# Two heads of a gated recurrence share one run of small matmuls, their starts are moved, and a later consumer takes three steps where it took four

## The chip, the cores and the metric

The kernel runs on one core of one Trainium2 chip. The metric is the device time in microseconds (us), the median of several runs; lower is better.

## The reference, cut to what matters

Two layers of a decoder trunk for a sequence of 256 tokens with 2048 features, in float32. Layer 0 mixes tokens with two mixers side by side, a gated MLP over chunks (gMLP, `y_a`) and a linear recurrence with forget gates (HGRN2, `y_b`); layer 1 is attention with forget gates; each layer ends in a gated MLP with a short convolution. The change touches layer 0's mixers alone:

```python
def hgrn2(q, f_logit, i, g, lower_bound, o_gain):          # 8 heads of 128
    log_f = logaddexp(log(lb), log1p(-lb) + log_sigmoid(fl))
    k = (1.0 - lb) * sigmoid(-fl)
    def step(state, xs):                                   # chunks of 64 tokens
        G = cumsum(lf_c, axis=2)
        o_inter = einsum('bhtk,bhkv->bhtv', q_c * exp(G), state)
        decay = exp(where(mask, G_t - G_s, -inf))
        scores = einsum('bhtk,bhtsk,bhsk->bhts', q_c, decay, k_c)
        o_intra = einsum('bhts,bhsv->bhtv', scores, v_c)
        new_state = exp(G_end) * state + einsum('bhsk,bhsv->bhkv', k_c * exp(G_end - G), v_c)
        return new_state, o_inter + o_intra
    return rms_norm(o, o_gain) * silu(g)

def mixer_ab(h, ...):
    u, v, q, f, i, g = split(h @ w_in, cuts)
    u, v = gelu(u), rms_norm(gelu(v), v_gain)
    mixed = einsum('hts,bcshd->bcthd', w_causal, v) + sp_b
    y_a = u * mixed
    y_b = hgrn2(q, f, i, g, lower_bound, o_gain)
    return concatenate([y_a, y_b]) @ w_out
```

## The kernel before

**Large products and steps.** Every weight matrix streams through the core once. `weights` (L190) loads a tile of 128 x 1024 numbers by SyncE's DMA queue into `w`, ScalarE rounds it into `wh` (L213), and VectorE subtracts to get the rest `wl` (L218). With the activations split the same way (`a`, later `ya` and `yb`), three matmuls of 512 columns take the place of one in full precision: L274 to L276 in `project_tok`, L294 to L296 in `project_four`. One such tile is twelve large matmuls on TensorE; this document calls it a step and numbers them from 1. There are four buffers of `w`, and three each of `wh` and `wl`, so ScalarE can be at most some two steps ahead of TensorE. The sums of a product lie in two PSUM banks (`pm`), one for each half of the tokens, and are evacuated by ScalarE when a product of eight steps is complete.

The order in layer 0: `w_v` (steps 1 to 16), then for each half of the heads `w_f`, `w_q`, `w_i` (eight steps each, to step 64), `w_u` (65 to 80), `w_g` (81 to 96), and the output product `w_abo` from step 97.

**Everything else rides along.** Work between the large products is written as Python generators. `tick()` (L138) runs once per step, ahead of its `weights`, and moves every live generator to its next `yield`; `after(n, g)` lets a generator begin n steps later; `start` begins one at once. So a `yield` is a step's wait, and what a generator records between two of them stands between the weight tiles of two steps in the engines' queues. A tile framework then orders the instructions of each engine and adds the semaphores; an engine executes its own in that order. `behind` and `add_manual_dep` hold an instruction behind another in that order without a semaphore. `mm_in` and `turn_in` are a matmul and a transpose on TensorE that stand behind the large matmuls handed over so far.

**A head of the recurrence, `hgrn(h)`** (L615). Instead of exponentials of sums it keeps products: the head's gates `l` and its keys and queries `t` (tile `kq`) are multiplied up level by level, for blocks of 1, 2, 4 ... 64 tokens. At each of the seven levels ScalarE copies the keys and queries as they stand into `E` (L633), and VectorE multiplies on (`kq`, `tot`; L637 to L644). The `yield`s in the loop spread this over three steps. Then on TensorE a cross product of two chunks (`xps`, 128 x 128) and two 64 x 64 products a level for the two groups of partitions (`levels`; one PSUM bank for even heads, one for odd). A step later ScalarE copies the cross product into `s128` (L659) and the first level into the head's state tile `st` (L662); VectorE masks the levels (`smk`, L664), sums them (`own`, L666), and writes `st` (L671). After some more steps a transpose of `st` on TensorE (L677 copies it out), and a step after that three products with the values `itok` (L166, L684, L685), whose squares, roots and scaled copies ScalarE and VectorE make (`so`).

`queries` (L694) starts the heads: for the j-th half and its i-th head it calls `after((4, 3)[j] * i + 1 - i // 2, hgrn(...))`; it has a `yield` behind every second head, so heads begin at its steps 1, 5, 9 and 13 in the first half, and 1, 4, 7 and 10 in the second.

**Around it.** `spatial(j, z)` (L754) is the gMLP: it waits until all eight heads are through (`left`), applies Gelu to the turned `w_u` product, and for each of four products multiplies and splits it into `ya`, with two `yield`s behind each. `gated` (L733) evacuates a `w_g` product with Silu into `zg`, multiplies by `itok`, and turns it with VectorE's transposes and 16 small DMAs into `yb`. `ya` and `yb` are what the output product reads.

ScalarE's functions come in tables; `act` loads one where the function's table is not the last one loaded (L98).

Of the kernel before, what the change touches and what calls it, by code (L numbers as in the profile page):

```python
# [11 lines left out]
AF = mybir.ActivationFunctionType  # L12
# [3 lines left out]
P = 128  # L16
HP = P // 2
# [17 lines left out]
AHEAD = {2: 2, 4: 4, 6: 6}  # L35
BEHIND = {6: 8, 8: 12}
LANE = 64
LEVELS = (64, 32, 16, 8, 4, 2, 1)
NL = len(LEVELS)
MCOLS = 2 * (NL + 1) * P  # L40
# [16 lines left out]
def tile_trunk(ctx: ExitStack, tc: tile.TileContext, x, pp_d, cst_d, mlev_d, msk_d,  # L57
               w_v, w_f, w_g, w_i, w_q, w_u, w_abo, w_cf, w_cqkv, w_cg, w_co, w_up, w_dn, spw_d, spb_d, out):
    nc = tc.nc
    V, SC, PE = nc.vector, nc.scalar, nc.tensor  # L60
# [15 lines left out]
    for c0, n in ((0, 1), (1, 1), (2, 1), (3, 1), (4, 2), (6, 2), (8, 4), (12, 4)):  # L76
        t = cp.tile([P, n, S], F32, tag=f"x{c0}", name=f"x{c0}")
        xload.append((t, c0, n))
        xT += [t[:, i] for i in range(n)]
    fetch = {c0: (t, x[:, c0:c0 + n, :]) for t, c0, n in xload}  # L80
    pp = cp.tile([P, -(-NPP // LANE) * LANE], F32, tag="pp", name="pp")
    cst = cp.tile([P, NK], F32, tag="cst", name="cst")
    ones = cp.tile([P, P], F32, tag="ones", name="ones")
    one1 = cp.tile([P, LANE], F32, tag="one1", name="one1")[:, 0:1]

# [6 lines left out]
    order = mybir.DependencyInfo(mybir.DependencyClass.NoSync, mybir.DependencyReason.DATA)  # L92
# [22 lines left out]
    def bank(tag="px"):  # L115
        n = nm(tag)
        return small["pool"].tile([P, 512], F32, tag=tag, name=n, bufs=small[tag])
# [22 lines left out]
    depth = [2]  # L140
# [6 lines left out]
    def after(n, g):  # L147
        soon.append([n, g])
# [16 lines left out]
    def mm_in(*args, **kw):  # L165
        return behind(PE.matmul(*args, **kw), "main")  # L166
# [179 lines left out]
    def rsq(dst, src, n):  # L346
        tag = "sq" if dst.shape[-1] == S else "rm"
        cols = dst.shape[-1] if dst.shape[-1] == S else LANE // math.prod(dst.shape[1:-1])
        m, t = (tp.tile(list(dst.shape[:-1]) + [max(cols, dst.shape[-1])], F32, tag=tag, name=nm(n_))
# [12 lines left out]
    class Norm:  # L362
# [30 lines left out]
        def finish_tok(self):  # L393
            p2 = bank()
            for T in range(2):
# [4 lines left out]
                yield  # L400
            Rt = cp.tile([P, LANE], F32, tag="Rt", name=nm("Rt"), bufs=2)[:, 0:2]
            rsq(Rt, p2[:, 0:4].rearrange("p (t two) -> p t two", two=2)[:, :, 0], D)
# [22 lines left out]
    def mixer_ab(norm):  # L425
# [3 lines left out]
        level = [bank("levels") for _ in range(2)]  # L429
# [60 lines left out]

        ss = hp.tile([P, LANE], F32, tag="ss", name="ss")

        def values():
# [7 lines left out]
            for li in range(1, NL):  # L501
                n = LEVELS[li]
                part = view(tri[:, 1], 0, (2 * n, 32 // n), (n - HP, 2), (1, n))
# [45 lines left out]
        gam = pp[:, C_GAM:C_GAM + 3 * NH]  # L549
        gm = hp.tile([P, LANE], F32, tag="gm", name="gm")  # L550
        mx, sm_, lb, omlb = (gm[:, i * NH:(i + 1) * NH] for i in range(4))
# [56 lines left out]
                yield  # L608

        yB = [None] * KT  # L610
        depth[0] = 3

        itoks, left = [], [NH]

        def hgrn(h):  # L615
            l, t = lf[h], kq[h]
            d0 = (h % 4) * P
            SC.activation(l, l, AF.Identity, bias=lb[:, h:h + 1], scale=omlb[:, h:h + 1])
            st = sts[h % 4]
            dg = hp.tile([P, 2, HP], F32, tag="dg", name=nm("dg"), bufs=4)  # L620
            V.tensor_tensor(dg, eye.unsqueeze(1).to_broadcast([P, 2, HP]),
                            dgc[:, h].unsqueeze(2).to_broadcast([P, 2, HP]), ALU.mult)
            yield

            V.tensor_tensor(t[:, 1::2], t[:, 1::2], view(l, P, (-P, 2), (1, P)), ALU.mult)
            E = hp.tile([P, NL, 2, P], F32, tag="E", name=nm("E"), bufs=2)
            tot = l
            tots = hp.tile([P, S], F32, tag="tot", name=nm("tot"), bufs=1)
            for li in reversed(range(NL)):
                n = LEVELS[li]  # L630
                m = P // n
                for sl in range(2):
                    SC.activation(E[:, li, sl].rearrange("p (b two n) -> p b two n", two=2, n=n),  # L633
                                  view(t, 2 * P * sl, (2 * n, 64 // n), (P + n, 2), (1, n)), AF.Copy)
                if not li:
                    ends = view(t, 0, (P + n, 2), (1, n))
                    V.tensor_tensor(ends, ends, view(tot, 1, (1, 2), (0, n)), ALU.mult)  # L637
                    break
                even = view(t, 0, (2 * P, 2), (2 * n, 64 // n), (1, n))
                odd = view(t, P + n, (2 * P, 2), (2 * n, 64 // n), (1, n))  # L640
                V.tensor_tensor(even, even, view(tot, 1, (m, 2), (2, m // 2), (0, n)), ALU.mult)
                V.tensor_tensor(odd, odd, view(tot, m, (-m, 2), (2, m // 2), (0, n)), ALU.mult)
                nt = tots[:, S - 2 * m:S - m]
                V.tensor_tensor(nt, view(tot, 0, (2, m)), view(tot, 1, (2, m)), ALU.mult)  # L644
                tot = nt
                if n in (4, 16):
                    yield
            yield
            xps = bank()
            mm_in(xps[:, 0:P], t[:, 0], t[:, 1], start=True, stop=True)  # L650
            i = h % 2
            for li in range(NL):
                for g in range(2):
                    k, q0 = slice(g * HP, (g + 1) * HP), (g if li else 1 - g) * HP
                    mm_in(level[i][k, li * HP:(li + 1) * HP], E[:, li, 0, k], E[:, li, 1, q0:q0 + HP],
                          start=True, stop=True)
            yield
            s128 = hp.tile([P, 2, P], F32, tag="s128", name=nm("s128"), bufs=2)
            SC.activation(s128[:, 0], xps[:, 0:P], AF.Copy)  # L659
            for g in range(2):  # L660
                k = slice(g * HP, (g + 1) * HP)
                SC.activation(st[k, g, HP - g * HP:P - g * HP], level[i][k, 0:HP], AF.Copy)  # L662
            smk = hp.tile([P, NL - 1, HP], F32, tag="smk", name=nm("smk"), bufs=1)
            V.tensor_tensor(smk, level[i][:, HP:NL * HP].rearrange("p (l c) -> p l c", l=NL - 1), msk, ALU.mult)  # L664
            own = hp.tile([P, HP], F32, tag="own", name=nm("own"))
            V.tensor_reduce(own, smk.rearrange("p l c -> p c l"), AX.X, ALU.add)  # L666
            both = smk[:, 0:2]
            V.tensor_tensor(both, own.unsqueeze(1).to_broadcast([P, 2, HP]), tri, ALU.mult)
            for g in range(2):
                k = slice(g * HP, (g + 1) * HP)  # L670
                V.tensor_tensor(st[k, :, k], both[k], dg[k], ALU.add)  # L671
            yield
            yield
            yield
            op = bank()
            turn_in(op[:, S:S + P], st[:, 1], ident)
            SC.activation(s128[:, 1], op[:, S:S + P], AF.Copy)  # L677
            yield
            while len(itoks) <= h // 4:
                yield  # L680
            itok = itoks[h // 4]
            i0, i1 = (itok[:, T, d0:d0 + P] for T in range(2))
            mm_in(op[:, 0:P], st[:, 0], i0, start=True, stop=True)
            PE.matmul(op[:, P:S], s128[:, 0], i0, start=True, stop=False)  # L684
            PE.matmul(op[:, P:S], s128[:, 1], i1, start=False, stop=True)  # L685
            so = hp.tile([P, LANE], F32, tag="so", name=nm("so"), bufs=2)[:, 0:2]
            for T in range(2):
                SC.activation(itok[:, T, d0:d0 + P], op[:, T * P:(T + 1) * P], AF.Square,
                              accum_out=so[:, T:T + 1])
            rsq(so, so, P)  # L690
            for T in range(2):
                SC.activation(itok[:, T, d0:d0 + P], op[:, T * P:(T + 1) * P], AF.Copy, scale=so[:, T:T + 1])
            left[0] -= 1

        def queries(j, z):
            while len(kq) < 4 * j + 4:
                yield
            for i in range(4):
                t = kq[4 * j + i]
                copy_in(view(t, 3 * P, (-2 * P, 2), (1, P)), natural(z[:, i]), AF.Copy)  # L700
                after((4, 3)[j] * i + 1 - i // 2, hgrn(4 * j + i))
                if i % 2:
                    yield

# [52 lines left out]
        def spatial(j, z):  # L757
            while left[0] or j and yB[4 * j - 1] is None:
                yield
            yield  # L760
            act_in(z, z, AF.Gelu)
            yield
            for i in range(4):
                b = 4 * j + i
                m = mg[b].rearrange("p (t n) -> p t n", t=2)
                sum_in(m, m, natural(z[:, i]), ALU.mult)
                yB[b] = quad("ya")
                split(yB[b], mg[b], turn=True)
                yield
                yield  # L770

        for j in range(2):
            after(LAG, spatial(j, turn(w_u[4 * j:4 * j + 4], late=True)))
# [477 lines left out]
```

## Time and profile before

| | |
|---|---|
| median of three runs | 2286.39 us (2286.0 to 2288.47) |
| the profiled execution's own time | 2287.58 us |
| its span, first to last instruction | 2285.8 us |
| TensorE (PE) busy | 2280.1 us |
| VectorE (DVE) busy | 1557.5 us |
| ScalarE (ACT) busy | 1315.6 us |
| GpSimd (POOL) busy | 421.2 us |
| mean granted TensorE clock | 1.000 |

How its lines are read. A row of the timeline has the start in us from the span's start, the duration in us, the engine, the line, the operation, what it writes `<-` what it reads, the shapes, how many such instructions follow each other (`x2`), and in brackets how long the engine was idle before it and what ended that wait. A row for a tile has the shortest, median and longest duration in ns. A row of a stage has its bounds and length, and then for each engine the busy us and the number of instructions, the granted clock, the DMA share and GB/s. A matmul in full precision shows as two passes. Matmuls overlap: their starts tell the pace, and their ends are modelled.

### The profile page before, as it was taken

The page shows a single profiled execution, that of the slowest core. Times are in us where ns is not written, and L with a number is a line of the kernel's source. Part 1 is how long each engine was busy: PE and PEld are TensorE (multiplying, and loading weights), DVE is VectorE, ACT ScalarE, POOL GpSimd, SP SyncE. Part 2 cuts the span into 40 slices and gives each one's busy share as a digit, 9 for nine tenths or more (in the row PEclk, how much of TensorE's full clock was granted, in tenths as well). Part 3 has the DMA queues.
Part 4 walks back from the last instruction along what each step waited for, and adds up shares of the span by engine and source line. Part 5 has one row for each costly group of instructions (what it writes and reads, how often), then busy time and mean ns, then how long its engine had stood idle before and what let it go on. Part 6 is the DMA issues. An engine that isn't in the chain of part 4 may idle for free.

```text
span 2285.8 us, 31588 instructions
## 1 busy us (share of the span) xinstructions
PE 2280.1 (100%) x10486; PEld 1895.1 (83%) x10486; DVE 1557.5 (68%) x2357; ACT 1315.6 (58%) x1973; POOL 421.2 (18%) x779
## 2 busy tenths in 40 slices
PE   9999999999999999999999999999999999999999
PEld 8888888888888888888888888888888888888887
DVE  7888667767467657766776675667776466667766
ACT  7578756656456445554555556655665455455642
POOL 0212232221012002201322211322311012012102
PEclk9999999999999999999999999999999999999999
DMA  8756677877667667765676656778777677666765
GB/s 282 217 171 195 198 217 217 243 223 216 201 194 233 208 202 217 214 215 175 186 232 211 194 178 193 209 224 242 224 218 218 195 210 217 208 210 212 223 203 175
DMA packets 487909, 481.07 MB, mean 210 GB/s; under 512 B 102880, under 2 KB 454640, under 8 KB 487744
## 3 DMA queue, kind: packets, MB, share of 16 engines
q1 hardware_dynamic: 460080, 448.42, 63.4%
q0 software_dynamic: 25360, 27.37, 5.0%
q10 hardware_dynamic: 2304, 3.26, 0.4%
q8 instruction: 82, 1.34, 0.3%
q14 instruction: 83, 0.68, 0.1%
HBM read 434.85 MB, written 2.12 MB: 191 GB/s over the span
## 4 chain that ended last, share of the span: by engine, by line
PE 99%; DMA 1%; SPq 0%; DVE 0%; ACT 0%; issue 0%; ACTq 0%
PE pm L294 27%; PE pm L295 27%; PE pm L296 27%; PE pm L275 5%; PE pm L274 5%; PE pm L276 5%; PE px L166 1%; PE pm L265 0%; PE px L811 0%; PE pm L812 0%; PE levels L166 0%; DMA w<-in_w_cqkv 0%; PE px L169 0%; DMA w<-in_w_v 0%; PE pm L239 0%; PE px L907 0%
## 5 line engine op out<-in xcount | busy, mean ns | idle before, releaser
L218 DVE TENSOR_TENSOR wl<-w,wh 128x1024 fp32r<-128x1024 f32 (+1 forms) x814 | 986.8, 1215 | 634.6 <-ACT wh L213 629.3
L213 ACT ACTIVATE wh<-w 128x1024 fp32r<-128x1024 f32 (+1 forms) x814 | 854.4, 1052 | 769.1 <-PE pm L296 552.2
L294 PE MATMUL pm<-wh,a 128*128 128x512 f32 x1792 | 700.4, 391 | 0.0
L296 PE MATMUL pm<-wh,a 128*128 128x512 f32 x1792 | 697.5, 389 | 0.0
L295 PE MATMUL pm<-wl,a 128*128 128x512 f32 x1792 | 697.4, 389 | 0.0
L320 POOL DMA_DIRECT2D zt<-tmp x413 | 224.2, 551 | 1198.7 <-DVE tmp L314 1050.5
L296 PEld LDWEIGHTS pm<-wh,a 128*128 128x128 f32 x1792 | 336.3, 188 | 70.4
L294 PEld LDWEIGHTS pm<-wh,a 128*128 128x128 f32 x1792 | 336.4, 188 | 69.9
L295 PEld LDWEIGHTS pm<-wl,a 128*128 128x128 f32 x1792 | 336.4, 188 | 69.4 <-DVE wl L218 0.4
L320 POOL DMA_DIRECT2D turn<-tmp x336 | 182.5, 551 | 545.4 <-DVE tmp L314 301.6
L294 PE MATMUL pm<-wh,hid 128*128 128x512 f32 x688 | 267.6, 389 | 0.0
L295 PE MATMUL pm<-wl,hid 128*128 128x512 f32 x688 | 267.6, 389 | 0.0
L296 PE MATMUL pm<-wh,hid 128*128 128x512 f32 x688 | 267.6, 389 | 0.0
L274 PE MATMUL pm<-wh,a 128*128 128x512 f32 x456 | 181.1, 398 | 0.3 <-ACT wh L213 0.3
L275 PE MATMUL pm<-wl,a 128*128 128x512 f32 x456 | 177.9, 390 | 0.8 <-DVE wl L218 0.8
L276 PE MATMUL pm<-wh,a 128*128 128x512 f32 x456 | 177.8, 390 | 0.0
L295 PEld LDWEIGHTS pm<-wl,hid 128*128 128x128 f32 x688 | 129.1, 188 | 26.9
L294 PEld LDWEIGHTS pm<-wh,hid 128*128 128x128 f32 x688 | 129.1, 188 | 26.8
L296 PEld LDWEIGHTS pm<-wh,hid 128*128 128x128 f32 x688 | 129.1, 188 | 26.8
L314 DVE STREAM_TRANSPOSE tmp<-z 128x512 f32<-128x512 f32 x132 | 91.8, 705 | 20.9 <-ACT z L1027 19.0
L160 ACT ACTIVATE conv<-zt,pp 128x256 f32<-128x256 f32 x176 | 95.3, 589 | 13.4 <-DMA zt<-tmp 8.9
L275 PEld LDWEIGHTS pm<-wl,a 128*128 128x128 f32 x456 | 85.7, 188 | 18.6 <-DVE wl L218 1.5
(227 smaller groups left out, 1918.8 us busy)
## 6 DMA issues: line engine op xcount, KB each, us to landing
w<-in_w_up SPq DMA_DIRECT2D x352, 512.0 KB, 4.5
w<-in_w_dn SPq DMA_DIRECT2D x176, 512.0 KB, 4.3
w<-in_w_cqkv SPq DMA_DIRECT2D x88, 512.0 KB, 4.3
w<-in_w_abo SPq DMA_DIRECT2D x32, 512.0 KB, 4.6
w<-in_w_cg SPq DMA_DIRECT2D x32, 512.0 KB, 4.1
w<-in_w_co SPq DMA_DIRECT2D x32, 512.0 KB, 4.5
zt<-tmp SPq DMA_DIRECT2D x414, 32.0 KB, 2.5
zt<-tmp POOLq DMA_DIRECT2D x413, 32.0 KB, 2.5
```

The costliest lines, as they stand in the source:

```text
L160: return behind(SC.activation(*args, **kw), "act")
L166: return behind(PE.matmul(*args, **kw), "main")
L213: deep["act"] = SC.activation(wh[:, p], w[:, p], AF.Copy)
L218: deep["sub"] = V.tensor_tensor(wl[:, p], w[:, p], wh[:, p].bitcast(F32), ALU.subtract)
L274: PE.matmul(ps[T], ah, h, start=k + i == 0, stop=False)
L275: PE.matmul(ps[T], ah, l, start=False, stop=False)
L276: deep["main"] = PE.matmul(ps[T], al, h, start=False, stop=k + i == KT - 1)
L294: PE.matmul(ps[T], ah, h, start=k + i == 0, stop=False)
L295: PE.matmul(ps[T], ah, l, start=False, stop=False)
L296: deep["mm"] = deep["main"] = PE.matmul(ps[T], al, h, start=False, stop=k + i == n - 1)
L314: V.transpose(tmp.rearrange("p (b m i t) -> p b m i t", b=4, m=4, t=2)[:, :, :, :, T], src(T).rearrange("p (m b j) -> p b m j", m=4, b=4))
L320: qs[(a + b) % len(qs)].dma_start(dst[BLK * b:BLK * (b + 1), :, a * n:(a + 1) * n], tmp[BLK * a:BLK * (a + 1), b * 4 * n:(b + 1) * 4 * n] ...
```

## The change

The cross products and level products of an even head and of the odd one after it are recorded together, in one run on TensorE, once both heads' levels are ready; both cross products go to one PSUM bank. Order dependencies keep the run in one piece: first the cross products, then the levels of the even head, then those of the odd. The odd head's consumers begin as before a step later. Heads begin at `START`, less one for the second pair because of the `yield` in `queries`: at 1, 3, 8 and 10 steps of `after`, in both halves alike. Up to four queued generators may be in flight where it was three (`depth`). In `spatial` the second `yield` behind a product is kept for every second product alone.

```diff
+START = ((1, 3, 9, 11), (1, 3, 9, 11))
...
-        depth[0] = 3
+        depth[0] = 4
...
+        made, crossed = {}, {}
 
         def hgrn(h):
...
             yield
-            xps = bank()
-            mm_in(xps[:, 0:P], t[:, 0], t[:, 1], start=True, stop=True)
+            made[h] = t, E
+            if h % 2 == 0:
+                while h + 1 not in made:
+                    yield
+                yield
+                xps = bank()
+                for i in range(2):
+                    ti = made[h + i][0]
+                    r = mm_in(xps[:, i * P:(i + 1) * P], ti[:, 0], ti[:, 1], start=True, stop=True)
+                    if i:
+                        tc.add_manual_dep(r.ins, last.ins.name, order, reason="one run")
+                    last = r
+                for i in range(2):
+                    Ei = made[h + i][1]
+                    for li in range(NL):
+                        for g in range(2):
+                            k, q0 = slice(g * HP, (g + 1) * HP), (g if li else 1 - g) * HP
+                            r = mm_in(level[i][k, li * HP:(li + 1) * HP], Ei[:, li, 0, k],
+                                      Ei[:, li, 1, q0:q0 + HP], start=True, stop=True)
+                            if not (li or g):
+                                tc.add_manual_dep(r.ins, last.ins.name, order, reason="one run")
+                    last = r
+                crossed[h] = crossed[h + 1] = xps
+            while h not in crossed:
+                yield
             i = h % 2
-            for li in range(NL):
-                for g in range(2):
-                    k, q0 = slice(g * HP, (g + 1) * HP), (g if li else 1 - g) * HP
-                    mm_in(level[i][k, li * HP:(li + 1) * HP], E[:, li, 0, k], E[:, li, 1, q0:q0 + HP],
-                          start=True, stop=True)
-            yield
             s128 = hp.tile([P, 2, P], F32, tag="s128", name=nm("s128"), bufs=2)
-            SC.activation(s128[:, 0], xps[:, 0:P], AF.Copy)
+            SC.activation(s128[:, 0], crossed[h][:, i * P:(i + 1) * P], AF.Copy)
+            if i:
+                yield
...
-                after((4, 3)[j] * i + 1 - i // 2, hgrn(4 * j + i))
+                after(START[j][i] - i // 2, hgrn(4 * j + i))
...
                 yB[b] = quad("ya")
                 split(yB[b], mg[b], turn=True)
                 yield
-                yield
+                if i % 2:
+                    yield
```

## The prediction

> **What bounds the kernel now.** I read the page, then the busy time by stage, then each engine's timeline around the recurrence. Busy times, the head of the chain of waits, and the stage that the change touches (128 to 258 us):
>
> ```profile
> span 2285.8 us, 31588 instructions
> PE 2280.1 (100%) x10486; PEld 1895.1 (83%) x10486; DVE 1557.5 (68%) x2357; ACT 1315.6 (58%) x1973; POOL 421.2 (18%) x779
> PE 99%; DMA 1%; SPq 0%; DVE 0%; ACT 0%; issue 0%; ACTq 0%
> ...
> 128.00:258.00 130.00, 130.00 (x790) 107.88 (x789) 103.03 (x272) 101.10 (x263) 26.02 (x48) 1.00 0.60 183
> ```
>
> TensorE sets the end: 99% of the chain, and 130.00 busy of 130.00 us in this stage, at a granted clock of 1.00. So the change can win only TensorE's own time, and it can lose whatever time it makes TensorE wait. The other two engines are not idle here (VectorE 103.03, ScalarE 101.10 of 130): they round and subtract each weight tile just before TensorE reads it. How close that is shows where it is closest, the weights of step 61 (a step is one weight tile, 12 large matmuls; I count them from the kernel's start), TensorE first and VectorE below:
>
> ```profile
> 181.79 0.39 PE L276 MATMUL pm<-wh,a 128*128 128x512 f32 x1
> 182.02 0.27 PE L169 MATMUL px<-cst,st 128*128 128x128 f32 x1
> 182.05 0.47 PE L274 MATMUL pm<-wh,a 128*128 128x512 f32 x1
> 182.36 0.39 PE L275 MATMUL pm<-wl,a 128*128 128x512 f32 x1
> 182.59 0.40 PE L276 MATMUL pm<-wh,a 128*128 128x512 f32 x1
> ```
>
> ```profile
> 180.59 1.23 DVE L218 TENSOR_TENSOR wl<-w,wh 128x1024 fp32r<-128x1024 f32 x1 [0.52 <-ACT wh L213]
> ```
>
> `wl` ends at 180.59 + 1.23 = 181.82 and is read at 182.36: 0.54 us in hand. Large matmuls start 0.227 us apart (181.79 to 182.02 is one of these), so a step takes 12 x 0.227 = 2.72 us.
>
> **The change part by part.** *What TensorE saves.* A head's run of small matmuls before, between two large ones:
>
> ```profile
> 130.02 0.39 PE L296 MATMUL pm<-wh,a 128*128 128x512 f32 x1
> 130.25 0.38 PE L166 MATMUL px<-kq 128*128 128x128 f32 x2
> 130.56 1.04 PE L166 MATMUL levels<-E 128*64 128x64 f32 x28
> 131.53 0.50 PE L294 MATMUL pm<-wh,a 128*128 128x512 f32 x1
> 131.87 0.40 PE L295 MATMUL pm<-wl,a 128*128 128x512 f32 x1
> ```
>
> and every level pass in the kernel:
>
> ```profile
> L166 PE MATMUL levels<-E x224: 222/222/271, 130.6 to 236.3; 128*64 128x64 f32 x112
> ```
>
> From large to large it takes 131.53 - 130.02 = 1.51 us, 1.28 more than the 0.227 of a plain pair; the first large one after it takes 0.34 until the next, 0.11 too much: 1.39 us per head. The cross product (2 passes) takes 0.31, the 28 level passes 0.97. Passes in mid-run are cheaper than their share: a transpose of the same shape ahead of a cross product costs 0.11 a pass (142.58 to 142.69, below), so of the 0.31 some 0.09 is the change of shape; and 28 passes lie 0.029 us apart on the mean (1.04 is from the first start to the last end, which is 0.22 long, so 0.82 / 28), so of the 0.97 some 0.15 is entry and exit. A pair's run then costs 4 x 0.11 + 0.09 + 56 x 0.029 + 0.15 + 0.11 = 2.42 us, against 2 x 1.39 = 2.78: 0.36 saved, 4 pairs, **-1.4 us**. Bounds: 0 if the second head pays everything again, -1.8 if also the output runs that now begin with a transpose save a shape change each.
>
> *Transposes* (L169). Before, three stand ahead of a cross product and five alone; after, four alone and four behind an output product. Alone: 182.05 - 181.79 - 0.227 = 0.03, plus 0.31 - 0.227 = 0.08 behind it, 0.11 together; in a run also 0.11:
>
> ```profile
> 142.35 0.39 PE L296 MATMUL pm<-wh,a 128*128 128x512 f32 x1
> 142.58 0.27 PE L169 MATMUL px<-cst,st 128*128 128x128 f32 x1
> 142.69 0.39 PE L166 MATMUL px<-kq 128*128 128x128 f32 x2
> ```
>
> So nothing. The instruction counts on every engine stay the same, save two table loads fewer on ScalarE, which is not in the chain.
>
> *What the other engines now do at once.* The order of instructions puts the pairs after steps 48, 56, 72 and 80 (the heads came after 44, 48, 52, 56 and 68, 71, 74, 77). Behind each pair VectorE has the masking, summing and state work of two heads within two weight tiles instead of one head's per three or four. First pair: VectorE and ScalarE of before at the same place (the evacuation after step 48):
>
> ```profile
> 142.78 0.69 ACT L580 ACTIVATE z<-pm,Rt 128x512 f32<-128x512 f32 x1 [0.50 <-PE pm L296]
> 143.37 0.27 ACT L677 ACTIVATE s<-px 128x128 f32<-128x128 f32 x1
> 143.53 1.06 ACT L102 ACTIVATE kt<-z 128x1024 f32<-128x1024 f32 x1
> 144.60 1.28 ACT L98 ACT_TABLE_LOAD   x1
> 145.90 0.28 ACT L659 ACTIVATE s<-px 128x128 f32<-128x128 f32 x1
> ```
>
> ```profile
> 144.62 1.23 DVE L711 TENSOR_TENSOR kt<-kt,orow 128x1024 f32<-128x1024 f32 x1 [0.40 <-ACT kt L102]
> 146.54 0.56 DVE L664 TENSOR_TENSOR smk<-levels,msk 128x384 f32<-128x384 f32 x1 [0.70 <-ACT st L662]
> 147.08 0.29 DVE L641 TENSOR_TENSOR kq<-kq,tot 128x128 f32<-128x128 f32 x1
> 147.28 0.85 DVE L666 TENSOR_REDUCE own<-smk 128x64 f32<-128x384 f32 x1
> 148.05 0.28 DVE L642 TENSOR_TENSOR kq<-kq,tot 128x128 f32<-128x128 f32 x1
> 148.25 0.28 DVE L668 TENSOR_TENSOR smk<-own,tri 128x128 f32<-128x128 f32 x1
> 148.45 1.22 DVE L218 TENSOR_TENSOR wl<-w,wh 128x1024 fp32r<-128x1024 f32 x1
> 149.59 0.28 DVE L671 TENSOR_TENSOR st<-smk,dg 64x128 f32<-64x128 f32 x1
> ```
>
> Let L be the start of step 48's last large matmul (142.35 above). The `orow` product starts at L + 2.27 as here (its input waits for the same evacuation). From start to start: `orow` 1.14 (my reading of a `wl` of the same size, 148.45 to 149.59), smk 0.54, kq 0.20, own 0.77, kq 0.20, smk 0.20: `wl` of step 51 starts at L + 5.3. Behind it in VectorE's queue stand, up to `wl` of step 52, itself (1.14), four st (0.30 each: a kq and the wait for its input), six kq, smk, own and the small smk: 1.14 + 1.2 + 1.2 + 0.5 + 0.77 + 0.2 = 5.0. That `wl` so ends at L + 5.3 + 5.0 + 1.2 = L + 11.5. TensorE wants it at L + 0.23 + 2.3 (pair) + 0.1 + 3 x 2.72 (steps 49 to 51) + 0.03 + 0.31 = L + 11.1 to 11.2. Late by about **0.3 us**. The bounds: 0 (each handover a little quicker), 1.4 when every instruction takes its full duration (second column) and none overlaps the next, 0.8 more in that stretch and 0.3 before it.
>
> The second pair (after step 56) comes with an evacuation as well: eight gate sums and two transposes, then a smk, ahead of `wl` of step 58, and own, two gates, small smk and two st ahead of `wl` of step 59. By the same count the first just holds and the second is late by **0.3** (0 to 1.2). The third (after step 72) has 20 instructions between the `wl` of steps 75 and 76, 6.8 us, with some 0.5 in hand: **0** (up to 0.6). The fourth has no level work of a later head beside it: 0.
>
> *The step past the recurrence.* The last output product now stands before step 86 (it was before step 83). Gated's first evacuation (`zg`) is the costly point: before, its two halves stood on ScalarE two weight tiles further on (behind `wh` of step 90); now the first half of step 88's sums stands ahead of `wh` of step 89, and on VectorE its product and its transpose stand ahead of `wl` of step 89. Such a `zg` later in the trace of before, TensorE, ScalarE and VectorE:
>
> ```profile
> 288.46 0.39 PE L296 MATMUL pm<-wh,a 128*128 128x512 f32 x1
> ```
>
> ```profile
> 288.89 0.69 ACT L102 ACTIVATE zg<-pm,Rt 128x512 f32<-128x512 f32 x1 [0.30 <-PE pm L296]
> 289.47 0.42 ACT L328 ACTIVATE ya<-mg 128x256 fp32r<-128x256 f32 x1
> ```
>
> ```profile
> 289.77 0.71 DVE L739 TENSOR_TENSOR zg<-zg,itok 128x512 f32<-128x512 f32 x1
> 290.37 0.44 DVE L330 TENSOR_TENSOR ya<-mg,ya 128x256 fp32r<-128x256 f32 x1
> 290.71 0.73 DVE L314 STREAM_TRANSPOSE tmp<-zg 128x512 f32<-128x512 f32 x1
> 291.34 0.67 DVE L739 TENSOR_TENSOR zg<-zg,itok 128x512 f32<-128x512 f32 x1
> ```
>
> The sixth large matmul of the step starts 5 x 0.227 = 1.13 into it, `zg` 0.43 later (288.46 to 288.89): 1.56; it ends at 2.25; product 0.60, transpose 0.63, `wl` 1.22: 4.7 us after step 88's start. TensorE wants this `wl` at 2.72 + 0.23 = 2.95: **1.8 us late**, by a chain that no lead can shorten, since it begins at TensorE's own sums. ScalarE adds to it: between `wh` of steps 88 and 89 it now has two squares, three small roots and copies, two table loads (1.30 each, 144.60 to 145.90), two copies, a Gelu as long as `kt` above (1.06), two `ya` and `zg`, 7 us against 8.2 us of three steps, and it comes to `zg` some 0.4 late: **2.2 us** (1.8 to 3.0).
>
> *The skip in gMLP's consumers.* Eight `ya` begin two weight tiles later on ScalarE (behind `wh` of step 88 for 86) and, with the step left out, end behind that of step 98 as before; they are wanted at steps 97 to 100, two a step: nothing. Without the shorter step the last would come two to four steps later and TensorE would stand at step 100; that cover is the edit's. Past step 100 all queues stand as before.
>
> [...]
>
> **The sum**: -1.4 + 0.3 + 0.3 + 2.2 = +1.4 us. The profiled execution took 2287.58 (span 2285.8 and 1.8 around it), so 2289.0; the median of the three runs, 2286.39, is 1.2 below it: **2287.8 us**. By the bounds, +0.0 (-1.8 + 1.8) to +6.2 (0 + 1.4 + 1.2 + 0.6 + 3.0).
>
> **The rivals.** *VectorE keeps up* (no wait at all, -1.4: 2285.0). For it: TensorE never waits in this stage before, with leads down to 0.54. Against it: step 89's chain starts at TensorE itself. *The bursts pile up* (slower): if VectorE's instructions don't overlap where two heads' work alternates with results that wait for each other, the bursts after pairs one to three cost 1.4, 1.2 and 0.6 and step 89 costs 3.0, -1.4 + 6.2 = +4.8: 2291.2. It decides from about 0.1 us more per instruction in the twenty of a burst. For it: the 0.70 that smk waited for ScalarE above; against it: kq after own started 0.77 after a reduction of 0.85. *The pair saves nothing* because the second head's levels pay the entry anew: +2.8, 2289.2. *Each table load holds ScalarE longer than its row*: two lie ahead of `zg`; with 1.3 more for each (as long again as the row's load), `wh` and `wl` of step 89 come 2.6 later: 2290.4. Against it: the row of 144.60. [...]
>
> **Chances.** Forecast 0.65, keeps up 0.13, bursts 0.16, nothing saved 0.04, table loads 0.02. A measurement of this kernel tells about 0.2% from no change, 4.6 us; only the bursts reach past it (2291.0), and with a little of the table case slower gets 0.17. No case saves 4.6 us; 0.02 for what I don't see. Same 0.81. The range, 2284.8 to 2291.2, holds the forecast, its neighbours down to no wait at all, and half of the bursts; the forecast's own is 2286.8 (no wait at steps 52 and 59, 1.8 at 89) to 2288.6 (3.0 at 89).
>
> **What would show it.** Right: four runs of 4 + 56 passes with about 2.3 us more than a plain gap; TensorE idle by about 2 us ahead of the second large matmul of step 89, ended by VectorE's `wl`; waits of some tenths at steps 52 and 59; nothing after step 100. Wrong: no idle time at step 89 (then a gain), waits over 1 us behind each pair (then the bursts), or a pair's run at 2.56 or more.

## The result, and the profile after

The changed kernel took 2290.02 us (median of 22 runs, 2288.48 to 2291.68), the kernel before 2286.59 (22 runs, 2285.62 to 2288.47): ratio 1.0014, 95% interval 1.0008 to 1.0020. It is slower by 3.4 us, 0.15%. The forecast was 2287.8, within 0.2% of before; its range (2284.8 to 2291.2) holds the time, the narrower one given for the forecast alone (2286.8 to 2288.6) does not.

The page of after, the span, the busy times and the head of its chain of waits:

```profile
span 2287.8 us, 31595 instructions
PE 2279.9 (100%) x10486; PEld 1895.0 (83%) x10486; DVE 1557.6 (68%) x2357; ACT 1313.5 (57%) x1971; POOL 420.1 (18%) x779
...
PE 97%; ACT 1%; DVE 1%; DMA 0%; issue 0%; SPq 0%; ACTq 0%; DVEq 0%
```

TensorE does the same 10486 instructions; ScalarE has two fewer, the table loads. New is one percent each of ScalarE and VectorE in the chain; before, both stood at 0%.

To find the places I took every pair of consecutive large matmuls between 20 and 300 us and added up what their starts lie apart beyond the plain distance of 0.2267 us (2.72 / 12): 22.58 us before, 26.08 after, **+3.50 us**. So the change's loss lies in this stretch. Below, this sum is called the stretch of 20 to 300 us. (The two profiled spans differ by less, 2.0, because the profile of before happened to wait 1.6 us for a weight transfer at 1127 us where that of after waited 0.5, with other small things outside the stretch.) By place:

| place | before to after, us | the prediction's term |
|---|---|---|
| small runs of TensorE (levels, cross, outputs, transposes) | -1.43 | -1.4, and 0 for transposes |
| step 52 | +0.60 | +0.3 |
| step 59 | +0.50 | +0.3 |
| step 89, two waits | +2.48 | +2.2 |
| step 89, slow matmuls behind them | +1.61 | none |
| all other gaps together | -0.26 | none |

A pair's run, TensorE's timeline of after:

```profile
140.44 0.39 PE L297 MATMUL pm<-wh,a 128*128 128x512 f32 x1
140.67 0.60 PE L167 MATMUL px<-kq 128*128 128x128 f32 x4
141.20 1.85 PE L167 MATMUL levels<-E 128*64 128x64 f32 x56
142.98 0.50 PE L295 MATMUL pm<-wh,a 128*128 128x512 f32 x1
143.32 0.40 PE L296 MATMUL pm<-wl,a 128*128 128x512 f32 x1
...
151.33 0.48 PE L295 MATMUL pm<-wh,a 128*128 128x512 f32 x1
152.13 0.50 PE L296 MATMUL pm<-wl,a 128*128 128x512 f32 x1 [0.33 <-DVE wl L219]
...
175.73 0.50 PE L276 MATMUL pm<-wl,a 128*128 128x512 f32 x1 [0.23 <-DVE wl L219]
```

From 140.44 to 142.98 there are 2.54 us, 2.32 over a plain gap, and 0.11 behind: 2.43 where 2.42 was worked out. At 152.13 and 175.73 the brackets show TensorE waiting for VectorE's `wl`. The bracket (0.33) is less than the delay (152.13 - 151.33 - 0.227 = 0.57), since the modelled end of the matmul before reaches into the gap. Of the 0.57, 0.09 belongs to a transpose just ahead (at 151.30) and is counted with the small runs in the table. The first large matmul after each of these stops takes 0.34 instead of 0.23 until the next one starts (152.13 to 152.47, 175.73 to 176.07), 0.11 more. So step 52 has 0.49 + 0.11 = 0.60, and step 59 in the same way 0.39 + 0.11 = 0.50.

Step 89, TensorE, ScalarE and VectorE of after (ahead of VectorE's rows the `wl` of step 52):

```profile
267.04 0.39 PE L297 MATMUL pm<-wh,a 128*128 128x512 f32 x1
268.45 0.73 PE L295 MATMUL pm<-wh,a 128*128 128x512 f32 x2 [1.02 <-ACT wh L214]
270.08 0.50 PE L296 MATMUL pm<-wl,a 128*128 128x512 f32 x1 [0.90 <-DVE wl L219]
...
270.74 0.63 PE L295 MATMUL pm<-wh,a 128*128 128x512 f32 x1
271.16 0.63 PE L296 MATMUL pm<-wl,a 128*128 128x512 f32 x1
...
274.07 0.40 PE L295 MATMUL pm<-wh,a 128*128 128x512 f32 x1
```

```profile
264.83 1.28 ACT L99 ACT_TABLE_LOAD   x1
266.12 0.76 ACT L329 ACTIVATE ya<-mg 128x256 fp32r<-128x256 f32 x2
266.78 0.67 ACT L103 ACTIVATE zg<-pm,Rt 128x512 f32<-128x512 f32 x1
267.35 1.04 ACT L214 ACTIVATE wh<-w 128x1024 fp32r<-128x1024 f32 x1
```

```profile
150.86 1.22 DVE L219 TENSOR_TENSOR wl<-w,wh 128x1024 fp32r<-128x1024 f32 x1
...
267.48 0.69 DVE L760 TENSOR_TENSOR zg<-zg,itok 128x512 f32<-128x512 f32 x1
268.21 0.71 DVE L315 STREAM_TRANSPOSE tmp<-zg 128x512 f32<-128x512 f32 x1
268.84 1.18 DVE L219 TENSOR_TENSOR wl<-w,wh 128x1024 fp32r<-128x1024 f32 x1
```

The order is the predicted one: `zg` stands ahead of `wh`, product and transpose ahead of `wl`. TensorE is late by 268.45 - 267.04 - 0.227 = 1.19 us for `wh`, and by 1.07 for `wl`, which here the third matmul of the step reads. What was not predicted follows: from 270.74 on each large matmul takes 0.43 us instead of 0.23, until 274.07. The stretches at which the clock is shown (the last four columns are POOL's busy time, the granted clock, the DMA share and GB/s; the first after the length is TensorE's busy time):

```profile
267.15:270.57 3.42, 1.50 (x6) 0.74 (x5) 3.25 (x6) 3.42 (x5) 0.00 (x0) 1.00 0.00 0
270.57:273.98 3.41, 3.41 (x10) 2.63 (x9) 3.41 (x6) 1.57 (x2) 0.00 (x0) 0.50 0.60 199
273.98:277.39 3.41, 3.41 (x16) 2.81 (x16) 1.89 (x4) 3.10 (x5) 2.65 (x5) 1.00 0.89 265
```

After a stretch with TensorE busy for 1.50 of 3.42 us the clock is exactly 0.50 for 3.41 us, then 1.00 again. Why the stretches are cut at these times, experiments 4 and 7 to 12 show.

### The profile page after: what moved, and what is told of

Same layout as the page of the kernel before. It is cut to its first block, busy times and chain, and to the rows that moved or that the text cites. A ratio compares the mean times of both kernels' runs of the same rounds, so it can differ in the third digit from the quotient of the medians.

```text
span 2287.8 us, 31595 instructions
## 1 busy us (share of the span) xinstructions
PE 2279.9 (100%) x10486; PEld 1895.0 (83%) x10486; DVE 1557.6 (68%) x2357; ACT 1313.5 (57%) x1971; POOL 420.1 (18%) x779
## 4 chain that ended last, share of the span: by engine, by line
PE 97%; ACT 1%; DVE 1%; DMA 0%; issue 0%; SPq 0%; ACTq 0%; DVEq 0%
PE pm L296 27%; PE pm L295 27%; PE pm L297 27%; PE pm L276 4%; PE pm L277 4%; PE pm L275 4%; PE px L167 1%; PE pm L266 0%; DVE wl L219 0%; ACT wh L214 0%; PE px L833 0%; PE px L170 0%; DMA w<-in_w_cqkv 0%; PE pm L834 0%; PE pm L240 0%
```

## The experiments

**1. The gated evacuation later.** The first `zg` is handed over three steps later, and its readers keep their place by three yields fewer:

```diff
         def gated(j, ps):
+            for _ in range(0 if j else 3):
+                yield
             z = big("zg")
...
-                act(z[:, c], ps[T], AF.Silu, scale=Rt[:, T:T + 1])
+                act_in(z[:, c], ps[T], AF.Silu, scale=Rt[:, T:T + 1])
...
-            for _ in range(LAG):
+            for _ in range(LAG - (0 if j else 3)):
                 yield
```

> The changed kernel, but the first gated evacuation (zg) is handed over three steps later, so that both its halves stand on ScalarE behind wh of step 91 and no longer ahead of wh of step 89. My theory: the loss is step 89, where TensorE first waits for wh (1.19 us), then for wl (1.07), and the granted clock then falls to 0.57 for some 3 us because of that idle time (8 to 9 large matmuls 0.427 us apart for 0.227: about 1.6 more). All three, 3.9 us together, go; what is left against the kernel before is -1.4 (four pair runs) +0.9 (waits at steps 52 and 59) = -0.5 us (-0.9 to 0): about 2286.1 where before is 2286.6. Rival A, the clock falls because of the denser small runs or by chance at that place, not because of the wait: the waits go, the slow matmuls stay, +1.1. Rival B, the evacuation only moves the wait on (wh and wl of step 92 or 93 late by about 2): no gain over the changed kernel, +3.4.

Measured: 2287.19 us beside 2286.46 of before (ratio 1.0001, 0.9992 to 1.0010). Step 89 on TensorE and on ScalarE:

```profile
266.93 0.39 PE L297 MATMUL pm<-wh,a 128*128 128x512 f32 x1
267.16 0.39 PE L295 MATMUL pm<-wh,a 128*128 128x512 f32 x1
267.38 0.39 PE L296 MATMUL pm<-wl,a 128*128 128x512 f32 x1
```

```profile
263.64 1.06 ACT L103 ACTIVATE turn<-turn 128x1024 f32<-128x1024 f32 x1
264.59 1.06 ACT L214 ACTIVATE wh<-w 128x1024 fp32r<-128x1024 f32 x1
```

`wh` follows the Gelu at once, starts 2.76 us earlier than in after, and no gap is left: both waits and the slow matmuls go together. The stretch of 20 to 300 us gives 22.73, +0.15 over before. I had expected -0.5: a wait of 0.55 (0.66 with the slow first matmul behind it) is new at step 99. All eleven runs have a granted clock of 1.000. So step 89 caused the loss, and rival A (clock by chance) falls. Rival B (the wait only moves on, +3.4) falls by its size, though 0.66 us of waiting did move on, to step 99.

**2. No merging.** Every head's cross and level products in their own run; the earlier starts, the depth of four and the shorter gMLP step stay:

```diff
-            made[h] = t, E
...
-                crossed[h] = crossed[h + 1] = xps
+            xps = bank()
+            mm_in(xps[:, 0:P], t[:, 0], t[:, 1], start=True, stop=True)
+            for li in range(NL):
...
-            SC.activation(s128[:, 0], crossed[h][:, i * P:(i + 1) * P], AF.Copy)
-            if i:
-                yield
+            SC.activation(s128[:, 0], xps[:, 0:P], AF.Copy)
```

> The changed kernel with each head's cross and level products in a run of their own again (start steps 1, 3, 8, 10, four generators in flight and the shorter gMLP step stay). My theory: without a partner to wait for, the recurrence ends earlier, zg stands behind wh of step 90 as before, and the small runs cost what they cost before: no wait at steps 52, 59 and 89, clock 1.00, time within 0.4 us of the kernel before (+0.0). Rival C, the earlier starts or the shorter gMLP step make the waits by themselves: waits at 52, 59 or 89 stay and it is 0.9 to 4 us above the kernel before.

Measured: 2287.68 beside 2286.46 (ratio 1.0005, 0.9996 to 1.0013); stretch 23.97, +1.39. No wait at 52, 59 or 89, as expected, but the kernel is not back at before. TensorE, at step 55:

```profile
163.62 0.39 PE L295 MATMUL pm<-wh,a 128*128 128x512 f32 x1
164.55 0.91 PE L167 MATMUL levels<-E 128*64 128x64 f32 x22 [0.54 <-ACT E L635]
165.60 0.49 PE L167 MATMUL px<-kq 128*128 128x128 f32 x2
...
166.40 0.50 PE L296 MATMUL pm<-wl,a 128*128 128x512 f32 x1
```

Most level products come ahead of the cross product here and wait for a copy `E` of ScalarE: 2.55 us over a plain gap where a head's run takes 1.39 with a transpose, 1.28 without. So the starts cost about 1.3 us by themselves in this form, at a place where the changed kernel has no wait. My 0.0 was wrong by that; rival C was right that the starts alone are not free, wrong about the places. The waits at 52, 59 and 89 come with the merging; whether they would come with the old starts too was not tried.

**3. Spread.** As the first, with the second heads of pairs one and two taking masks, sums and state three steps later:

```diff
-            if i:
+            for _ in range(i + (3 if h in (1, 3) else 0)):
                 yield
...
-            V.tensor_tensor(smk, level[i][:, HP:NL * HP].rearrange("p (l c) -> p l c", l=NL - 1), msk, ALU.mult)
+            (sum_in if h in (1, 3) else V.tensor_tensor)(smk, level[i][:, HP:NL * HP].rearrange("p (l c) -> p l c", l=NL - 1), msk, ALU.mult)
```

> As the one with the late gated evacuation, and the second heads of pairs one and two also take their levels' masking, sums and state three steps later, behind wl of step 52 (and 60), so that VectorE has one head's work at a time there. My theory: the waits at steps 52 and 59 (0.49 and 0.45 us) are VectorE's alone and go; what is left is the pair runs' saving, -1.4 us against the kernel before (-1.0 to -1.6): about 2285.2. Rival D, the waits go to another weight tile a few steps on (VectorE has the same work in the same 20 us): -0.5, as without the spread.

Measured: 2286.70 beside 2286.46 (ratio 1.0001, 0.9992 to 1.0010); stretch 22.66, no better than the first. TensorE:

```profile
164.20 0.50 PE L296 MATMUL pm<-wl,a 128*128 128x512 f32 x1 [0.43 <-DVE wl L219]
```

The waits at steps 52 and 59 are gone and one of 0.60 stands in step 56 instead (163.38 to 164.20), and the one at step 99 has grown from 0.55 to 0.93. Rival D was right.

**5 and 6. Two smaller moves.** In 5, `zg` is two steps later instead of three, and since the three yields fewer behind it stay, its readers come one step earlier than in 1. In 6 also a first pair runs one step later: the expectation says the first pair of each four, but the edit (`h in (0,)`) moves that of the first four heads alone.

```diff
-            for _ in range(0 if j else 3):
+            for _ in range(0 if j else 2):
...
                 while h + 1 not in made:
                     yield
-                yield
+                for _ in range(2 if h in (0,) else 1):
+                    yield
```

> The changed kernel with the gated evacuation two steps later instead of three (both halves on ScalarE behind wh of step 89) and three yields fewer behind it. It tells whether the wait of 0.55 us that was left at step 99 in the version with three comes from the late evacuation: there the yb copies waited 0.96 us for the transfer behind zg's transpose. My theory: no wait at step 89 (the evacuation of step 88's sums is then behind the weights of 89), the transfer lands about 4 us earlier, no wait at step 99, and the stretch of 20 to 300 us is 0.5 us shorter than before (-1.44 + 0.9). Rival: wl of step 90 is now late behind two zg products and a transpose (about 0.5 to 1), and nothing is won over the version with three.

> As the one with the evacuation two steps later, and the first pair of each four takes its merged run one step later, so that the keys' evacuation (two transposes and the orow product, 2.4 us of VectorE) is done before the pair's masks and sums. My theory: the waits at steps 52 and 59 are only VectorE having both at once; with one step between them that of step 52 (0.49) goes, that of 59 stays or shrinks, and the stretch is 1.0 to 1.4 us shorter than before. Rival: VectorE has too little time over the whole 20 us, the wait moves to step 53 to 56 with the same 0.5 us.

Measured: 2287.43 and 2289.96 beside 2286.34 (ratios 1.0004, 0.9995 to 1.0013, and 1.0016, 1.0007 to 1.0025); stretches 23.36 and 25.22. In 5 the wait has moved one step on, to step 90, TensorE and VectorE:

```profile
270.47 0.73 PE L295 MATMUL pm<-wh,a 128*128 128x512 f32 x2
272.00 0.50 PE L296 MATMUL pm<-wl,a 128*128 128x512 f32 x1 [0.80 <-DVE wl L219]
```

```profile
268.92 1.29 DVE L762 TENSOR_TENSOR zg<-zg,itok 128x512 f32<-128x512 f32 x2 [0.75 <-ACT zg L103]
270.13 0.70 DVE L315 STREAM_TRANSPOSE tmp<-zg 128x512 f32<-128x512 f32 x1
270.76 1.18 DVE L219 TENSOR_TENSOR wl<-w,wh 128x1024 fp32r<-128x1024 f32 x1
```

Two products and a transpose stand ahead of `wl` of step 90: 0.97 us, the rival's case; the wait at step 99 shrinks to 0.15 with the slow first matmul. In 6 step 52 is free of waiting, but the pair's work now meets the queries' evacuation, and TensorE waits at steps 58 and 59:

```profile
173.75 0.73 PE L275 MATMUL pm<-wh,a 128*128 128x512 f32 x2 [1.05 <-ACT wh L214]
175.01 0.50 PE L276 MATMUL pm<-wl,a 128*128 128x512 f32 x1 [0.53 <-DVE wl L219]
...
178.25 0.50 PE L276 MATMUL pm<-wl,a 128*128 128x512 f32 x1 [0.18 <-DVE wl L219]
```

These are 1.21, 0.69 and 0.35 us, where the changed kernel waits 0.39; and in five of the eleven runs of 6 the granted clock is below 1.000 (0.998 or 0.999). Both expectations failed: each of the three moves tried in the 20 us behind the first pair (3 and 6) or at step 89 (5) took one wait away and put another a few steps on.

**4, 7, 8, 9. The clock.** The kernel before, with extra small products of VectorE (0.32 us each) ahead of `wl` of some weight tiles of the first FFN, so that TensorE waits there. The first probe, 4, has twelve such tiles; 7 has fourteen, with 16 to 19 products and one with 26; 8 and 9 have four, with 17 to 28:

```diff
+EXTRA = {170 + 16 * i: 14 + 3 * i for i in range(12)}
...
-            deep["sub"] = V.tensor_tensor(wl[:, p], w[:, p], wh[:, p].bitcast(F32), ALU.subtract)
+            tiles[0] += 1
+            for _ in range(EXTRA.get(tiles[0], 0)):
+                r = V.tensor_tensor(ones, ones, ones, ALU.mult)
+                tc.add_manual_dep(r.ins, deep["sub"].ins.name, order, reason="probe")
+                deep["sub"] = r
+            r = V.tensor_tensor(wl[:, p], w[:, p], wh[:, p].bitcast(F32), ALU.subtract)
+            if tiles[0] in EXTRA:
+                tc.add_manual_dep(r.ins, deep["sub"].ins.name, order, reason="probe")
+            deep["sub"] = r
```

> The kernel before, with 14, 17, ... 47 extra small VectorE products ahead of wl of twelve weight tiles of the first FFN, 16 tiles apart, so that TensorE waits from nothing to some 6 us at twelve places: it measures after which idle time matmuls run slow. My theory: idle times up to about 1.5 us leave the granted clock at 1.00, those of 2 us and more are followed by some 8 large matmuls about 0.43 us apart instead of 0.23, costing about 1.6 us each; the table of idle time against slow matmuls has a step between 1.2 and 2.5 us. Rival E, the slow matmuls of step 89 do not come from the idle time: waits of 2 to 3 us are followed by matmuls 0.23 apart, or only far longer ones slow the clock.

> The second clock probe: 16 to 19 extra VectorE products (0.32 us each) ahead of wl of fourteen weight tiles of the first FFN, for idle times of TensorE between 0.8 and 2.6 us. In the first probe, waits of 0.77 and 0.85 us were followed by full speed and those of 2.57 us and more by 7 to 11 large matmuls 0.43 us apart, as many after 2.6 us as after 14. My theory: there is one bound between 1.2 (the pair of 0.56 and 1.03 in the kernel before, 1.16 in the version without merging, all at full speed) and 2.3 us; below it nothing follows, above it 1.4 to 2.2 us are added whatever the wait's length. Rival: the loss grows with the idle time between (fewer slow matmuls after shorter waits), so that a wait of 1.5 us costs about half.

> Third clock probe: 17, 20, 18 and 27 extra VectorE products (0.32 us each) ahead of wl of four weight tiles of the first FFN that lie where the first probe gave 0.85 us with 14, 0.77 with 17, 2.81 with 20 and 2.57 with 29: so single waits of about 1.8, 1.7, 2.2 and 1.9 us. The second probe gave waits of 0.42 to 0.52 and one of 4.56, nothing between. My theory: one bound, by the waits seen so far between 1.2 and 2.57 us; the shortest wait followed by large matmuls 0.43 us apart and the longest one at full speed now close it in, and above it 7 to 11 slow ones follow whatever the length. Rival: waits of 1.7 to 2.2 us are followed by fewer slow matmuls (2 to 5), so that the loss grows with the wait.

> As the third clock probe with 18, 21, 17 and 28 products: single waits of about 2.1, 2.1, 1.9 and 2.25 us. Same theory and rival.

Measured: most waits came out shorter than 0.9 or longer than 4.5 us; none lies between 1.2 and 2.57, so the single bound I looked for was not closed in. All that were 0.85 or less, and one of 1.18, were followed by full speed; those of 2.57 and more by 7 to 13 matmuls 0.427 us apart, with no relation to the length (12 after 7.4 us, 7 after 13.6). An order shows in the times at which the slow stretches end. In the first probe, worked out from TensorE's starts:

```
end of slow stretch, us   655.238  709.856  761.043  812.246  863.447  921.465  979.491  1040.937
to the one before, us               54.618   51.187   51.203   51.201   58.018   58.026    61.446
divided by 3.413                      16.00    15.00    15.00    15.00    17.00    17.00     18.00
```

From the first end to the last there are 385.699 us, 113 x 3.413: in this probe the ends lie on a grid of 3.413 us. An interval of it is called a window below. Cut along it, the wait of 2.81 us of the first probe, and the wait of 1.18 us of the fourth:

```profile
648.41:651.83 3.42, 0.87 (x4) 0.38 (x2) 3.18 (x10) 2.97 (x5) 0.00 (x0) 1.00 0.49 154
651.83:655.24 3.41, 3.32 (x8) 2.64 (x9) 3.41 (x7) 0.47 (x2) 0.00 (x0) 0.50 0.58 170
```

```profile
515.68:519.10 3.42, 2.40 (x11) 1.66 (x11) 3.29 (x7) 2.04 (x3) 0.00 (x0) 1.00 0.57 172
519.10:522.51 3.41, 3.41 (x17) 2.80 (x16) 3.41 (x8) 1.15 (x2) 0.00 (x0) 1.00 0.78 235
```

Behind a window with TensorE busy for 0.87 of 3.42 us came one at a clock of 0.50, behind one busy for 2.40 us one at 1.00. The second probe has two windows with busy times between these, one at full clock with its follower, and one at half clock:

```profile
409.49:412.90 3.41, 1.57 (x7) 0.95 (x6) 3.14 (x10) 1.06 (x1) 0.00 (x0) 1.00 0.12 41
412.90:416.32 3.42, 0.61 (x3) 0.53 (x4) 3.32 (x7) 0.00 (x0) 0.00 (x0) 1.00 0.47 151
```

```profile
464.10:467.51 3.41, 2.26 (x5) 1.82 (x6) 3.41 (x6) 0.42 (x1) 0.00 (x0) 0.50 0.37 119
```

The window at full clock busy for 1.57 us was followed by 1.00. The one at half clock busy for 2.26 us was not: the next window, 467.51 to 470.92, ran at 0.50 again. So the busy time alone does not order these windows; what else counts was not tested.

Behind a wait of 4.8 us in the second probe the clock did not fall at the restart: TensorE went on at 415.70 at full speed and turned slow at about 416.35 (starts at 415.70, 416.04, 416.27, 416.65, then 0.427 apart), where by the later ends of that probe a window begins. In the changed kernel, at step 89, it was a window busy for 1.50 us, with most of two waits of 1.19 and 1.07 us in it, that stood ahead of one at 0.50.

**10 to 12. The changed kernel again.** Three more profiles of the changed kernel, nothing edited.

> The changed kernel once more, for a second profile of step 89. In the probes the slow stretches end on a grid of 3.413 us (eight ends of the first probe), and a grid window with 2.2 us of idle time or more is followed by a slow one, windows with up to 1.2 us are not; the grid lies elsewhere against the kernel's start in every execution. My theory: the waits of step 89 stay as they were (1.19 + 1.07 us, within 2.8 us), but whether one window holds enough of them depends on where the grid falls: in some executions the slow stretch of 1.6 us is missing. By windows set at random both waits fall whole into one window in 18% of executions, and at least 1.7 us of them in about 50%. Rival: the clock follows the waits themselves, so every execution has the same 8 to 9 slow matmuls.

> The changed kernel a third time; same theory and rival as the second.

> The changed kernel a fourth time; same theory and rival as the second.

Measured: the waits are 1.19 and 1.07 in all three. Number 12 has the slow stretch, 10 and 11 have not: two of four with the profile above. The timed runs say the same: of after's 22, ten have a granted clock of 0.999 (median 2290.51 us) and twelve 1.000 (2289.36). In number 11 the grid is taken from a slow stretch at the kernel's start (four large matmuls take 2.05 us from 4.92 on, where in after they take 1.19 from 4.63 on; it ends at 6.93, 77 x 3.413 before 269.73), and falls between the two waits:

```profile
266.32:269.73 3.41, 2.38 (x11) 1.46 (x9) 2.26 (x6) 3.40 (x7) 0.00 (x0) 1.00 0.00 0
269.73:273.15 3.42, 2.52 (x11) 1.97 (x11) 3.42 (x5) 3.14 (x3) 0.00 (x0) 1.00 0.37 112
```

One wait in each window, 2.38 and 2.52 us busy, and the clock stays at 1.00. The rival, that the clock follows the waits alone, falls. In number 10 the stretch at the kernel's start ends at 4.81, so that a window runs from 267.64 to 271.05: it holds most of both waits, TensorE is busy for 1.86 us in it, and the clock stays at 1.00.

But the time hardly fell: the stretch of 20 to 300 us is 25.44 and 25.37 in 10 and 11, 26.11 in 12, so 0.7 us came back, not 1.6. The rest is lost later. Number 10, TensorE at step 97, and ScalarE:

```profile
292.20 0.50 PE L296 MATMUL pm<-wl,ya 128*128 128x512 f32 x1 [0.40 <-DVE wl L219]
```

```profile
283.49 1.06 ACT L214 ACTIVATE wh<-w 128x1024 fp32r<-128x1024 f32 x1 [1.34 <-PE pm L297]
287.26 2.67 ACT L161 ACTIVATE yb<-turn,pp 128x256 fp32r<-128x256 f32 x4 [2.71 <-DMA turn<-tmp]
```

ScalarE stands 2.71 us for the transfer that turns `zg`; four copies and the `wh` of steps 97 and 98 are queued behind, and TensorE waits 0.57 at step 97 and 0.05 at 99 (0.85 with the slow first matmuls; 0.73 in number 11). The transfer's issues on SyncE, in before and in number 10 (the last two times are the first and the last start; GpSimd's twelve begin 0.5 and 0.2 us behind):

```profile
L320 SPq DMA_DIRECT2D turn<-tmp x4: 591/598/602, 271.2 to 273.1; - x4
```

```profile
L321 SPq DMA_DIRECT2D turn<-tmp x4: 591/602/621, 274.4 to 276.3; - x4
```

They start 3 us later, while `yb` keeps its place behind `wh` of step 96. One of the three is `zg`'s second transpose, which stands behind two `wl` now and ends at 272.23 instead of 271.17. The other two pass before the first issue: ahead of it in SyncE's queue stands a weight load that starts at 273.70, when VectorE has done the next `wl` (273.67). In after, with the slow stretch, the same four copies start at 286.18 without a wait. Number 10 differs from it in two ways: ScalarE does the `wh` ahead of them 1.7 us earlier (283.49 for 285.22), because TensorE is earlier, and the transfer lands at least 1.1 us later (287.26 for 286.18). The first follows from the missing slow stretch. Why the transfer lands later, in number 11 as in 10, is not shown.

## Why the prediction came out as it did

*What bounds the kernel:* right. Nothing but TensorE's own time was won, and every loss is TensorE waiting for a weight tile, or slow behind such a wait.

*What TensorE saves* (-1.4): right, -1.43, with the entry and exit paid once a run as worked out. "The pair saves nothing" is excluded. *Transposes* (0): right.

*Steps 52 and 59* (0.3 and 0.3): right in place and engine, 0.60 and 0.50 in size. `wl` of step 52 ended at 150.86 + 1.22 = 152.08, 11.64 behind L = 140.44, where 11.5 was counted; the matmul follows 0.05 later; the rest is the 0.11 that a first matmul after a stop loses, which the prediction knew from the runs of small matmuls and didn't add to its waits. "The bursts pile up" (1.4 and 1.2) did not happen: behind the third and fourth pair there is no wait at all.

*Step 89* (2.2, bounds 1.8 to 3.0): right in size, 2.26 us of waiting and 0.23 behind the two stops, but not in form. The prediction had one wait of about 2 us for `wl`, ahead of the second matmul; there are two, 1.19 for `wh` ahead of the first and 1.07 for `wl` ahead of the third. ScalarE was later than counted: `zg` started at 266.78, 0.7 us behind the point 1.56 us into step 88 (267.04 + 0.23 - 2.72 = 264.55), where 0.4 was counted, and `wh` of step 89, which stands behind it, is a wait of its own that the prediction did not list. Each of the two table loads ahead of `zg` let the next instruction start 1.29 us later (261.94 to 263.23, 264.83 to 266.12), so "each table load holds ScalarE longer" is excluded.

*The sum* is the step that failed: it adds the waits and takes all else as unchanged. The waits came out 0.8 larger together (0.60 + 0.50 + 2.48 = 3.58 for 2.8), and two terms were missing. After 2.26 us of waiting within 2.81 us, two of the four profiles show one window of 3.41 us at half clock, 1.61 us. The other two lose 0.85 and 0.73 us at steps 97 and 99. "*Past step 100 all queues stand as before*" was true of the order but said nothing of steps 96 to 99, where the transfer that follows from the late `zg` was left without its 3 us. With the measured waits and either term the stretch of 20 to 300 us is +2.8 to +3.5 instead of +1.4, and the median's +3.43 fits it. That 2290.02 lies in the wide range is luck: its upper half was there for the bursts, which did not happen, and what was missing were larger waits and two terms that the prediction did not have.

*The skip in gMLP's consumers* (0): no wait in steps 97 to 100 of the changed kernel is for `ya`. Whether TensorE would wait there without the skip was not tried.

What would mend it is not settled. With `zg` three steps later the loss is gone and the time is that of before, but the -1.43 is eaten by steps 52, 59 and 99. None of the versions was measurably faster than before, and 6 was slower.

## What to carry to other kernels

When an edit makes a full engine wait, price the wait, the slower first instruction behind it (0.11 us here), and what the late engine's results feed next: here a late evacuation made a late transpose, a late transfer and, in numbers 10 and 11, a loss of 0.85 and 0.73 us at steps 97 and 99. Two waits close together can cost more than their sum: those of 1.19 and 1.07 us, within 2.81 us, were followed in two of four profiles by a window of 3.41 us at a clock of 0.50, which cost 1.61 us more. And where two engines have little spare time over 20 us, moving a burst by one or three steps can merely move the wait, as in 3, 5 and 6; that no place is free of it is not shown.

## What was not expected of the hardware

The slow stretches of the first probe ended on a grid of 3.413 us (eight ends), and where the grid falls differs from execution to execution: near step 89 a window began at 270.57 in the profile of after, at 271.05, 269.73 and 270.59 in numbers 10, 11 and 12. So a fixed program lost 1.6 us at that place in some executions and not in others. Of the windows at full clock above, those busy for 0.87 and 1.50 us were followed by a clock of 0.50, those busy for 1.57, 1.86, 2.38, 2.40 and 2.52 us by 1.00; the one at half clock busy for 2.26 us was still followed by 0.50. Busy times rest on modelled ends (0.39 us for a large matmul, with starts 0.227 apart), so by my estimate they are no closer than some tenths, and what the clock goes by stays open. At full clock a stop of TensorE between two large matmuls cost 0.11 us beyond its length (0.34 instead of 0.23 to the next start), after 0.39 us at step 59 as after 1.19 at step 89.
